# Attention and the sample's recurrent state, woven into fewer halves of the gate projections

## The chip, the cores and the metric

The kernel runs on one core of a Trainium2 chip. The metric is the time of one launch on the device in microseconds; for one core this is the core's own time. The time before is the median of three runs. The profile shows one further execution of the same program, with its own time.

## The reference: one decoder layer for a prompt and a sample

One layer is computed for a prompt of 512 tokens and for a sample of 8 sequences with 4 tokens each, both with the same weights, all in f32. Cut to its steps:

```python
z = x @ w_in + b_in                       # one projection, columns split among all mixers
qm, km, vm, og, ig, fg, qs, ks, vs, ga, gb = split(z)
h, C, n, m = mlstm_mix(...)               # recurrent matrix memory, 4 heads of 128 x 256
ya = head_norm(h) * sigmoid(og)
yb, k, v   = swa(...)                     # sliding window of 128, 16 query and 4 key heads of 64
mix = (sigmoid(ga) * (ya @ w_a) + sigmoid(gb) * (yb @ w_b)) @ w_out
x = LN1(alpha*x + mix)
x = LN2(alpha*x + moe(x))                 # 32 experts in 4 groups, two of them per token
x = LN3(alpha*x + sigmoid(x @ w_pg) * (p @ w_pp))
```

The prompt begins with an empty memory; the sample brings eight states C of 4 x 128 x 256 and windows of keys and values, and returns them updated. In local attention a query of the prompt sees its own block of 128 keys and the one before it (the first block sees itself alone), with a bias and a sink in the softmax.

## The kernel before

**Jobs.** A dense product with a weight matrix is cut into jobs of 256 columns. A job's weights come in one DMA of 1 MB (`fetch`, line 727) into `raw` and are split by ACT and DVE into a rounded part `wH` and a rest `wL` (lines 592 and 593, `split_from`). Three matmuls with f32r operands (`three`, lines 709 to 711) stand for one f32 product. In a "column" job each of two units holds 128 columns, and its product runs over the tokens in two halves, 0 to 255 and 256 to 543 (the second has the 32 sample tokens too), with 24 matmuls per half into a PSUM tile `pj`. After each half `done` moves the result out: for ga and gb DVE (line 881) takes the first half and ACT (line 879) the second, into `sigA` and `sigB`. The weights of a unit are split while the unit before it runs. ga and gb are four jobs each, so together 8 jobs, 16 units, 32 halves. Afterwards come the jobs of w_a, w_b and w_out.

**Weaving.** `stream` is a generator that yields after every half. `weave(upto, (generator, rate), ...)` advances it half by half; after each half every other generator gets its rate added to a counter and is resumed once for each whole number in it. So a rate of 2.6 writes 2.6 pieces of that work behind each half. When the jobs are done, what is left is written in turn.

**What is woven into ga and gb.** Two generators:

- `swa()`, the prompt's local attention: 16 units, for two pairs of key heads, four blocks of queries and two pairs of heads. For a unit, `stack` splits the queries (lines 1333, 1334), `scores` multiplies them with the keys into two PSUM tiles `tp` (lines 1350, 1352), DVE adds the bias and takes the maximum (line 1355), ACT takes the exponential (line 1367), and POOL divides by the sum (line 1373) in `lg`, which has two buffers. `values` turns the result on TensorE into a tile `nm` (line 1385), copies it to `pT` (lines 1388, 1390), multiplies it with the values into a tile `sp` (line 1397), and ACT copies the result over the queries (line 1399). The scores of a unit are written before the values of the one before it.
- `sample_mlstm()`, the sample's recurrence: a prelude, then for each of eight sequences b0 to b7 a load of its state `Cb` (512 KB, line 1419, on POOL's queue, two buffers), products with it into a tile `sp` (line 1490), four updates through tiles `tp` and `nm` (lines 1495 to 1498), and a store of the state (line 1501, POOL's queue). The ending turns the normaliser (line 1504), norms the result and multiplies it into the sample's columns of `ya` (lines 1512, 1514).

The PSUM tiles `tp`, `nm`, `sp` and `pj` have two buffers each, and are shared by all of these.

**What follows.** `early.close()` ends the pools of the projections' inputs, of the attention and of the sample's states. Then the sigmoids of `sigA` (line 1521) are written, then the split of `ya` into `yaH` and `yaL` (nine pieces on ACT and on DVE, lines 592 and 593 again), and then the jobs of w_a, which read them, with the sample's attention woven in.

**The order of the instructions.** The written order is not yet that of the engines. When the program is built, a planner plays it through with its own costs and deals the instructions out to the engines: an engine that is free takes, of those that are ready, the one written first. On the chip each engine keeps that order. Buffers of a pool with the same name are handed out in the written order.

Of the kernel before, what the change touches and what calls it, by code (L numbers as in the profile page):

```python
# [544 lines left out]
def tile_decoder_step(ctx: ExitStack, tc: tile.TileContext, *aps):  # L545
# [4 lines left out]
    def pool(name, bufs=1, side="left", space=None, stack=ctx):  # L550
        if space is None:
            return stack.enter_context(tc.tile_pool(name=name, bufs=bufs, side=side, reuse_waits="tile"))
        return stack.enter_context(tc.tile_pool(name=name, bufs=bufs, space=space))
# [260 lines left out]
    def weave(upto, *others):  # L814

        nonlocal flow
        others = [[g, rate, 0.0, True] for g, rate in others]
        while state["done"] < upto:
            next(flow)
            for o in others:  # L820
                o[2] += o[1]
                while o[3] and o[2] >= 1.0:
                    o[2] -= 1.0
                    o[3] = next(o[0], "end") != "end"
        if state["pending"]:
            state["pending"]()
            state["pending"] = None
        live = [o for o in others if o[3]]
        while live:
            live = [o for o in live if next(o[0], "end") != "end"]  # L830
# [134 lines left out]
    N_GA, N_GB, N_WA, N_WB, N_WO = 22, 26, 30, 34, 38  # L965
# [344 lines left out]
    sws = early.enter_context(ExitStack())  # L1310
# [202 lines left out]
        gated = ya[:, :, SEQ:].rearrange("p (h e) s -> p e h s", e=2)  # L1513
        dve.tensor_tensor(out=gated, in0=pt[:].rearrange("p e (h s) -> p e h s", h=MH), in1=gated, op=ALU.mult)

    weave(N_GB, (swa(), 2.6), (sample_mlstm(pool("smp", stack=sws)), 1.1))
    early.close()

    def sigmoids(g):
# [947 lines left out]
```

## Time and profile before

| | |
|---|---|
| median of three runs | 1100.4 us (1099.33 to 1101.43) |
| the profiled execution's own time | 1102.54 us |
| its span, first to last instruction | 1100.6 us |
| TensorE busy, matmuls | 1003.2 us, 91% |
| VectorE (DVE) / ScalarE (ACT) / GpSimd (POOL) busy | 512.0 / 369.0 / 255.7 us |
| granted TensorE clock, mean | 0.966 |
| DMA | 256.45 MB, mean 233 GB/s |

The span is cut into stages by what the jobs do. The projections of q, k, v and so on end at about 280 us; ga and gb run from there to about 430 us; w_a begins at 443.0 us; the experts' weights are streamed from about 558 us on, at some 426 GB/s in the middle of the experts' phase. The profile's lines have an engine, the line of the kernel, the operation, the tile written and the tiles read. TensorE's weight loads (PEld) overlap its matmuls. Behind an instruction stands how long its engine was idle before it and what it was waiting for.

### The profile page before, as it was taken

To read this page: it belongs to the slowest core of one execution; us is meant where nothing else is said; L and a number is where in the kernel's file an instruction comes from. 1 tells how busy PE (TensorE), PEld (TensorE's weight loads), DVE (VectorE), ACT (ScalarE), POOL (GpSimd) and SP (SyncE) were. 2 spreads that over 40 slices of the span, in tenths; PEclk is the share of its full clock that TensorE was granted. 3 is DMA by queue.
4 is the path that set the end of the run, shared out by engine and by line. 5 is a ranking of instruction groups with operands and counts; after the bars stand their busy time and mean duration, and the time that the engine had idled before them with its cause. 6 is when DMAs were issued, how large, how long until landed. Compare 5 with 4: busy or idle time off the path is not lost.

```text
span 1100.6 us, 26984 instructions
## 1 busy us (share of the span) xinstructions
PE 1003.2 (91%) x10269; PEld 823.1 (75%) x10270; DVE 512.0 (47%) x1308; ACT 369.0 (34%) x751; POOL 255.7 (23%) x385
## 2 busy tenths in 40 slices
PE   9999999999999998999999976875988888986987
PEld 8988999999988886899989634553556565654775
DVE  5555533645767765565566731111122222222696
ACT  5311224533677776523321311110111111223531
POOL 6000000501355555312410211111222222221011
PEclk9999999999999998999999988999899999999699
DMA  8321322222515423534379889999999999979701
GB/s 257 78 78 54 101 77 77 67 68 85 159 46 184 156 97 122 183 93 137 109 278 407 339 307 393 426 427 426 426 427 426 427 426 427 426 319 400 291 34 63
DMA packets 90892, 256.45 MB, mean 233 GB/s; under 512 B 11115, under 2 KB 58433, under 8 KB 70820
## 3 DMA queue, kind: packets, MB, share of 16 engines
q1 hardware_dynamic: 76036, 224.61, 52.9%
q0 software_dynamic: 10272, 27.21, 7.0%
q10 hardware_dynamic: 4512, 3.64, 1.1%
q8 instruction: 49, 0.80, 0.3%
q14 instruction: 23, 0.19, 0.1%
HBM read 241.89 MB, written 19.61 MB: 238 GB/s over the span
## 4 chain that ended last, share of the span: by engine, by line
PE 77%; DMA 7%; issue 6%; SPq 4%; DVE 4%; ACT 1%; POOL 1%; DVEq 0%; ACTq 0%; POOLq 0%
PE pj L709 14%; PE pj L710 14%; PE pj L711 13%; PE psG L306 13%; PE kept L318 6%; SPq L137 3%; DMA gu3b<-in_w_eu_dram 2%; DMA w<-in_w_pg_dram 2%; SPq L143 1%; PE sp L1397 1%; PE psX L298 1%; PE nm L1385 1%; PE sp L767 1%; DMA wg_in<-in_w_in_dram 1%; PE pp L2267 1%
## 5 line engine op out<-in xcount | busy, mean ns | idle before, releaser
L709 PE MATMUL pj<-xH,wH 128*128 128x256 f32 (+1 forms) x672 | 197.4, 294 | 0.0
L710 PE MATMUL pj<-xL,wH 128*128 128x256 f32 (+1 forms) x672 | 196.1, 292 | 0.0
L711 PE MATMUL pj<-xH,wL 128*128 128x256 f32 (+1 forms) x672 | 194.7, 290 | 0.0
L592 ACT CAST wH<-raw 128x1024 fp32r<-128x1024 f32 x76 | 79.6, 1048 | 200.5 <-PE pj L710 127.1
L709 PEld LDWEIGHTS pj<-xH,wH 128*128 128x128 f32 x672 | 126.5, 188 | 4.6 <-issue 3.7
L710 PEld LDWEIGHTS pj<-xL,wH 128*128 128x128 f32 x672 | 126.4, 188 | 2.2 <-issue 1.6
L711 PEld LDWEIGHTS pj<-xH,wL 128*128 128x128 f32 x672 | 126.2, 188 | 2.1 <-issue 1.9
L593 DVE TENSOR_TENSOR wL<-raw,wH 128x1024 fp32r<-128x1024 f32 x76 | 95.4, 1256 | 64.7 <-ACT wH L592 64.5
L474 DVE COPY xT<-xg 128x256 f32 x48 | 14.4, 299 | 224.6 <-PE psG L306 224.6
L306 PE MATMUL psG<-w,xT 128*32 128x256 f32 x1408 | 87.0, 401 | 28.6 <-issue 23.2
L306 PEld LDWEIGHTS psG<-w,xT 128*32 128x32 f32 x1408 | 53.6, 115 | 60.0 <-issue 39.0
L440 ACT ACTIVATE both<-psG 128x128 f32<-128x128 f32 x49 | 13.6, 278 | 242.9 <-PE psG L306 242.9
L1373 POOL TENSOR_SCALAR lg<-lg,sm 128x256 f32<-128x256 f32 (+1 forms) x64 | 59.0, 934 | 44.9 <-DVE sm L1370 34.7
L265 POOL DMA_INDIRECT ybuf<-ysb,idy x48 | 47.6, 991 | 43.6 <-POOL idy L262 39.6
L426 ACT ACTIVATE xg<-psX,gcol 128x128 f32 (+1 forms) x100 | 36.3, 467 | 51.4 <-PE psX L298 51.4
L709 PE MATMUL pj<-wH,xH 128*128 128x256 f32 x160 | 46.8, 292 | 1.0 <-DVE vs L923 1.0
L318 PE MATMUL kept<-w,hT 128*32 128x256 f32 x704 | 44.2, 390 | 2.5 <-DVE hT L479 2.5
L710 PE MATMUL pj<-wL,xH 128*128 128x256 f32 x160 | 44.4, 277 | 0.0
L711 PE MATMUL pj<-wH,xL 128*128 128x256 f32 x160 | 44.3, 277 | 0.0
L306 PE MATMUL psG<-gu3a,xT 128*32 128x256 f32 x480 | 30.7, 398 | 14.7 <-issue 6.7
L479 DVE STREAM_TRANSPOSE hT<-both 128x128 f32<-128x128 f32 x49 | 20.1, 409 | 45.4 <-PE kept L318 45.0
L306 PE MATMUL psG<-w2a,xT 128*32 128x256 f32 x384 | 26.6, 423 | 15.9 <-issue 12.8
(655 smaller groups left out, 2281.4 us busy)
## 6 DMA issues: line engine op xcount, KB each, us to landing
w<-in_w_eg_dram SPq DMA_DIRECT2D x24, 1024.0 KB, 24.9
w<-in_w_eu_dram SPq DMA_DIRECT2D x24, 1024.0 KB, 27.2
w<-in_w_ed_dram SPq DMA_DIRECT2D x24, 1024.0 KB, 27.4
raw<-in_w_in_dram SPq DMA_DIRECT2D x22, 1024.0 KB
r_p<-in_w_ed_dram SPq DMA_DIRECT2D x14, 1024.0 KB, 24.5
w2a<-in_w_eg_dram SPq DMA_DIRECT2D x7, 1024.0 KB, 20.0
w2a<-in_w_eu_dram SPq DMA_DIRECT2D x7, 1024.0 KB, 22.4
w2b<-in_w_eg_dram SPq DMA_DIRECT2D x7, 1024.0 KB, 23.6
```

The costliest lines, as they stand in the source:

```text
L137: return [eng.dma_start(out=W[s][half][:, i], in_=w[i][bass.ds(e, 1)].rearrange("a (p k) f -> (a p) k f", p=P)[:, ks]) for i in range(2)]
L265: gp.indirect_dma_start(out=ybuf.rearrange("t (q d) -> (t q) d", q=4), out_offset=bass.IndirectOffsetOnAxis(ap=idy[:, r:r + 1], axis=0), i ...
L306: m = pe.matmul(psG[32 * q:32 * q + 32], xT[:, k], W[s][half][:, :, kh, P * q:P * q + P], start=k == 0, stop=k == KD - 1)
L318: m = pe.matmul(out[32 * q:32 * q + 32], hT[:, 32 * k:32 * k + 32], W[s][2][k // 2][:, k % 2, 256 * q:256 * q + 256], start=k == 0, stop=k ...
L426: m = act.activation(out=out, in_=psX[:, k], func=AF.Identity, bias=gcol[:, 1, k:k + 1], scale=gcol[:, 0, k:k + 1])
L479: dve.transpose(out=hT[:].rearrange("p (r t) -> p r t", r=4), in_=h[:].rearrange("p (f r) -> p r f", r=4)).then_inc(S["ch"], 1)
L592: act.copy(out=H, in_=src)
L593: return eng.tensor_tensor(out=L, in0=src, in1=H.bitcast(F32), op=ALU.subtract)
L709: pe.matmul(out, lh(k), rh(k), start=start and i == 0, stop=False)
L710: pe.matmul(out, lh(k), rl(k), start=False, stop=False)
L711: pe.matmul(out, ll(k), rh(k), start=False, stop=stop and i == len(ks) - 1)
L1373: gp.tensor_scalar(out=lg[:, par, j, 0:nk], in0=lg[:, par, j, 0:nk], scalar1=sm[:, 2, par, j:j + 1], scalar2=None, op0=ALU.mult)
```

## The change

Only the two rates of one call are changed.

```diff
-    weave(N_GB, (swa(), 2.6), (sample_mlstm(pool("smp", stack=sws)), 1.1))
+    weave(N_GB, (swa(), 3.2), (sample_mlstm(pool("smp", stack=sws)), 1.2))
```

`swa()` yields 60 times and `sample_mlstm()` 21 times, so it takes 22 resumptions to run the sample to its end. Counted so, the last piece of attention was written behind half 24 and is now behind half 19 of 32, and the last of the sample was behind half 20 and is now behind half 19. (The change's own summary counts 23 and 22, and 19 and 20.) As the two rates grow by different shares, the order of the pieces among each other changes too. What is computed, the instructions, the buffers and the transfers stay as they were.

## The prediction

> **What bounds the kernel now.** I read the views in this order: the page for the shares, the busy time by stretch around the place of the change, TensorE's timeline where that stage ends, and the timelines of ACT and DVE at the same place. First the page.
>
> ```profile
> span 1100.6 us, 26984 instructions
> PE 1003.2 (91%) x10269; PEld 823.1 (75%) x10270; DVE 512.0 (47%) x1308; ACT 369.0 (34%) x751; POOL 255.7 (23%) x385
> ```
>
> TensorE is busy nearly throughout, so what counts is where it is not. By stretches (span, then busy time of each engine, the granted clock, DMA):
>
> ```profile
> 282.00:430.00 148.00, 148.00 (x1171) 129.86 (x1170) 98.35 (x336) 107.91 (x268) 76.52 (x100) 1.00 0.37 119
> 430.00:437.00 7.00, 2.60 (x20) 1.65 (x20) 3.27 (x11) 6.37 (x14) 4.03 (x5) 0.83 0.45 152
> 437.00:443.00 6.00, 4.44 (x20) 2.45 (x20) 0.82 (x2) 1.90 (x5) 6.00 (x12) 0.63 0.72 227
> 443.00:449.00 6.00, 5.63 (x30) 5.25 (x31) 6.00 (x11) 6.00 (x13) 3.22 (x6) 0.72 0.18 49
> ```
>
> From 282 to 430 us the gate projections ga and gb run with attention and states woven in, and TensorE never stands still. Then come 19 us in which it idles, and in which the clock falls to 0.63 and 0.72. TensorE's timeline says why (start, length, line, operation, idle time before):
>
> ```profile
> 430.20 0.29 PE L711 MATMUL pj<-xH,wL 128*128 128x288 f32 x1
> ...
> 433.36 0.65 PE L1397 MATMUL sp<-pT,vs 128*64 128x256 f32 x4 [1.33 <-DVE pT L1390]
> ...
> 440.44 1.57 PE L1397 MATMUL sp<-pT,vs 128*64 128x256 f32 x8 [0.57 <-DVE pT L1390]
> 443.02 0.38 PE L709 MATMUL pj<-yaH,wH 128*128 128x256 f32 x1 [1.01 <-ACT yaH L592]
> ...
> 449.38 0.30 PE L710 MATMUL pj<-yaL,wH 128*128 128x288 f32 x1
> ...
> 453.33 0.39 PE L709 MATMUL pj<-yaH,wH 128*128 128x256 f32 x1
> ...
> 456.29 0.29 PE L709 MATMUL pj<-yaH,wH 128*128 128x288 f32 x1
> ```
>
> The last gb matmul starts at 430.20. The last two attention units still have their transposes (L1385) and value products (L1397) to do, each behind another engine, until 440.44 + 1.57 = 442.0. Only then does w_a begin, at 443.02; its first half lasts until 449.38, 6.4 us, where a later half takes 456.29 - 453.33 = 3.0 us. What lies between is the split of ya:
>
> ```profile
> 442.06 0.37 ACT L1399 COPY qsT<-sp 128x256 f32<-128x256 f32 x1 [1.51 <-PE sp L1397]
> 442.35 4.57 ACT L592 CAST yaH<-ya 128x512 fp32r<-128x512 f32 x9
> 443.00 5.24 DVE L593 TENSOR_TENSOR yaL<-ya,yaH 128x512 fp32r<-128x512 f32 x9 [2.49 <-ACT yaH L592]
> ```
>
> Its casts follow on ACT right behind the attention's last copy: the tiles are opened after the attention's pools are closed. So the stage ends with a bare chain, and every microsecond by which attention (and the states, for yaL) end earlier is worth up to one, until gb itself is the end.
>
> **The change, part by part.** It adds no instruction, DMA or wait and removes none; two rates change what is written beside what. Counted from the generators' yields, attention has 60 pieces and the sample 22 resumptions. At 2.6 and 1.1 per half the last of them lie in halves 24 and 20 of 32; at 3.2 and 1.2 both lie in half 19.
>
> *Does the written place set the time?* Mostly not. One half takes 148.0 / 32 = 4.6 us. The scores of the last unit (call the units S0 to S15) are written in half 21, some 50 us before the end, but run in the last one. These are the first score matmuls of S4, S6, S9, S10, S11, S12, S14 and S15:
>
> ```profile
> 309.37 0.28 PE L1350 MATMUL tp<-kd,q 128*128 128x256 f32 x1
> 332.07 0.28 PE L1350 MATMUL tp<-kd,q 128*128 128x256 f32 x1
> 363.58 0.22 PE L1350 MATMUL tp<-kd,q 128*128 128x128 f32 x1
> 377.29 0.28 PE L1350 MATMUL tp<-kd,q 128*128 128x256 f32 x1
> 381.05 0.28 PE L1350 MATMUL tp<-kd,q 128*128 128x256 f32 x1
> 389.96 0.28 PE L1350 MATMUL tp<-kd,q 128*128 128x256 f32 x1
> 418.85 0.28 PE L1350 MATMUL tp<-kd,q 128*128 128x256 f32 x1
> 427.27 0.28 PE L1350 MATMUL tp<-kd,q 128*128 128x256 f32 x1
> ```
>
> The attention is about 50 us behind its place, so in any contest with the projections it already comes first; writing it still earlier wins nothing directly. What the rates do change is the order between units and states. Both take PSUM tiles with the same names (tp, nm, sp, two buffers each), handed out in written order, so a state written ahead of a unit holds that unit up. Written before: S4 b0 S5 S6 b1 S7 b2 S8 b3 S9 b4 S10 S11 b5 S12 b6 S13 b7 S14, the sample's ending, S15. After: S4 S5 b0 S6 b1 S7 S8 b2 S9 S10 b3 S11 b4 S12 b5 S13 S14 b6 S15 b7, ending. So b7 and the sample's ending move from ahead of S15 to behind it.
>
> *The price of a state in that queue.* S4 to S6 is two units and one state in 22.7 us, S9 to S11 the same in 17.5, mean 20.1. S11 to S14 is three of each in 37.8, 12.6 per pair. So a unit costs 20.1 - 12.6 = 7.5 and a state 5.1. Test: eleven units and eight states would make 123 us, and S4 to S15 took 117.9. Bounds: S10 and S11, with no state between them, are 3.8 us apart; if every unit cost that, a state would cost (117.9 - 41.8) / 8 = 9.5; if states rode free, 0. I take 5.1, nearest to the rows that mix both. The sample's ending lies between S14 and S15, 8.4 us apart: 8.4 - 7.5 = 0.9. S15 thus moves from 427.3 to 427.3 - 6.0 = 421.3, bounds 417 and 426.
>
> *The tail.* From S15 to the last value product it took 442.0 - 427.3 = 14.7, and 1.0 more to w_a. That gives 421.3 + 15.7 = 437.0 in place of 443.0: 6.0 us.
>
> *What now lies behind S15.* b7 and the ending, whose C_s store must land before yaL may use that memory. The nearest pattern (a unit, then a state straight behind it) is S8 with b3, the widest S12 with b6; S8's first score, then DVE's last update of b3, of b6 and of b7, ya's sample columns, and POOL's store of b3:
>
> ```profile
> 355.47 0.22 PE L1350 MATMUL tp<-kd,q 128*128 128x128 f32 x1
> 363.01 0.47 DVE L1498 SCALAR_TENSOR_TENSOR Cb<-Cb,win,nm 128x257 f32<-128x257 f32 x1
> 406.81 0.48 DVE L1498 SCALAR_TENSOR_TENSOR Cb<-Cb,win,nm 128x257 f32<-128x257 f32 x1 [1.02 <-PE nm L1497]
> 418.12 0.48 DVE L1498 SCALAR_TENSOR_TENSOR Cb<-Cb,win,nm 128x257 f32<-128x257 f32 x1 [0.40 <-PE nm L1497]
> 425.80 0.41 DVE L1514 TENSOR_TENSOR ya<-tp,ya 128x256 f32<-128x256 f32 x1
> 364.69 0.80 POOL L1501 DMA_DIRECT2D out_dram<-Cb  x1
> out_dram<-Cb POOLq DMA_DIRECT2D x8, 512.0 KB, 3.4
> ```
>
> Near pattern: update at 363.0, 7.5 after S8, store issued at 364.7, landed 3.4 later, 12.6 after S8. Behind a S15 at 421.3 that is 433.9, before the attention's end (436.0). The sample's columns follow their last update by 7.7: 421.3 + 7.5 + 7.7 = 436.5, needed only by w_a's second half. So this lies beside the tail and costs nothing; if the cover goes it costs what the slower rival below says. Behind a waiting load of a state on POOL's queue stands the normalising of the next unit (L1373); fewer states between units makes that rarer, and I count 0 for it.
>
> *How far it can go.* What TensorE did after 430.4 has to be done anyway, only earlier: eight transposes and eight value products for each of two units, and two small transposes. The chain of waits has their price at full clock (start, length, what):
>
> ```profile
> 410.39 0.22 PE nm L1385 x2
> 424.46 0.58 PE sp L1397 x4
> ```
>
> 18 x 0.11 + 16 x 0.145 = 4.3 us. So w_a cannot begin before 434.7.
>
> *w_a's first half.* 6.4 us now. DVE's nine pieces in 5.24 us set 8 x 0.58 = 4.7 for a first half that waits for its split at full clock. Saved between 0 and 1.7; the gap before w_a would shrink from 12.6 to 6.6 us with 4.3 of work in it, so I take 1.0.
> The Trainium skill (TensorE: Matmul & The Clock Gate, Part 1: The HAM clock gate) has the array's clock halved after an idle window of about 3.4 us and restored after as long of steady work. The trace agrees: 0.63, and still 0.72 in six well-filled microseconds. By that rule a gap of 2.3 us need not halve the clock at all, and the sum would be 7.7 in place of 7.0.
>
> *Sum:* 6.0 + 1.0 = 7.0 us off the profiled execution's 1102.5 (its span 1100.6 and 1.9 around it). The median of the runs, 1100.4, stands 2.1 below that execution; I take the same 7.0 off it: **1093.4**. Does it reach the end? TensorE is full in the last stretch of the dense part, and the experts' weight loads are first issued from memory that the dense part frees:
>
> ```profile
> 560.00:580.00 20.00, 20.00 (x177) 16.50 (x178) 12.27 (x25) 3.04 (x3) 0.00 (x0) 1.00 1.03 410
> 557.92 0.37 SPq L1760 DMA_DIRECT2D w<-in_w_eg_dram  x1
> ```
>
> So the whole later part moves with it; I count all of it.
>
> **The rivals.** *Hidden whole:* a state costs near its upper bound, or the written place counts after all; S15 comes at 417 or before, the attention ends before gb, w_a starts at 434.7 with its split done. 443.0 - 434.7 = 8.3, and the first half falls from 6.4 to about 3.9 (3.0 and eight transposes of 0.11): 10.8 us, 1089.6. For it: the 3.8 us spacing. Against: the lag of 50 us under either rate.
>
> *No effect:* states ride free and S15 stays near 426; the new tail ends at 441 or 442. 1099 to 1101. For it: each unit's own chain over two buffers could be all that paces. Against: 17.5 and 22.7 us for two units with a state, beside 3.8 for one without.
>
> *Slower, the sample becomes the last:* S15 stays at 427.3 and b7 behind it takes the widest pattern, S12 to b6's update: 406.8 - 390.0 = 16.8. Store issued 1.7 and landed 3.4 later: 449.2, and the split of ya starts there instead of at 442.35, 6.9 us later: 1107.3. It decides from the point where the store lands after 442.35, which at this spacing is S15 later than 420.4, at the near spacing (12.6) later than 429.7. For it: the ending, which was hidden ahead of S15, is now the last in line. Against: it needs both the unmoved S15 and the wide spacing.
>
> **How the numbers follow.** Forecast 0.52, hidden whole 0.15, no effect 0.14, slower 0.19. The likeliest's own range is 1090 to 1098 (S15 from 418 to 425). The range to record reaches past hidden whole and half-way into the slower case: 1088.5 to 1103. A measurement of this kernel can tell about 0.2%, 2.2 us, from no change. Faster: 0.52 + 0.15 = 0.67; same 0.14; slower 0.19.
>
> **What would show it.** Right: the last unit's scores start near 421 with b7's products behind them; the last L1397 ends near 436; the stretch from gb's last matmul to w_a's first is a few us with less than 3 idle; gb's last matmul comes slightly later than 430.2. Wrong: S15 unmoved relative to gb's end; yaH or yaL waiting for the store of Cb; TensorE idle inside ga and gb, because casts of weights stand behind denser attention; or a later stage that takes the gain back.

## The result, and the profile after

The changed kernel takes 1091.35 us (median of 12 runs, 1088.87 to 1097.63) against 1100.54 (12 runs, 1098.63 to 1103.94): a ratio of 0.9916, with a 95% interval from 0.9900 to 0.9932. The forecast was 1093.4. The profiled execution took 1091.46 us, its span is 1089.6, 11.0 under the one before.

The page of the changed kernel (share of the span and instructions per engine):

```profile
span 1089.6 us, 26983 instructions
PE 995.5 (91%) x10269; PEld 818.1 (75%) x10270; DVE 510.3 (47%) x1308; ACT 367.0 (34%) x749; POOL 253.8 (23%) x385
```

The same stretches (span, then busy time of each engine, granted clock, DMA), now up to the end of gb, for the first half of w_a, and for w_a behind that:

```profile
282.00:433.00 151.00, 150.56 (x1205) 132.42 (x1205) 99.93 (x344) 110.46 (x281) 79.37 (x105) 1.00 0.37 117
433.00:439.00 6.00, 5.46 (x28) 3.59 (x28) 5.46 (x10) 6.00 (x12) 5.68 (x11) 1.00 0.68 223
438.90:494.10 55.20, 55.20 (x506) 52.06 (x506) 30.34 (x50) 16.88 (x23) 10.00 (x17) 1.00 0.55 170
```

The bare 13 us in which the clock had fallen are gone: gb runs to 433, three microseconds longer than before, since the attention's work now lies under it, and w_a follows at full clock. TensorE's timeline has the first scores of S4, S14 and S15, the last value products, the last matmul of gb, then w_a and its second half:

```profile
306.25 0.28 PE L1350 MATMUL tp<-kd,q 128*128 128x256 f32 x1
...
396.50 0.38 PE L1350 MATMUL tp<-kd,q 128*128 128x256 f32 x1
...
408.58 0.28 PE L1350 MATMUL tp<-kd,q 128*128 128x256 f32 x1
...
431.45 1.08 PE L1397 MATMUL sp<-pT,vs 128*64 128x256 f32 x8
...
432.96 0.29 PE L711 MATMUL pj<-xH,wL 128*128 128x288 f32 x1
...
433.56 0.38 PE L709 MATMUL pj<-yaH,wH 128*128 128x256 f32 x1 [0.20 <-ACT yaH L592]
...
438.86 0.40 PE L709 MATMUL pj<-yaH,wH 128*128 128x288 f32 x1
...
551.37 0.31 PE L1783 MATMUL sp<-wrb,onesf 128*128 128x36 f32 x2
```

S15's scores moved from 427.27 to 408.58, 18.7 us, three times the forecast. Its last value product ends at 432.5, 23.9 behind its scores instead of 14.7. w_a starts at 433.56 instead of 443.02: 9.5 us, which is all there was, as gb's own last matmul is at 432.96. Of the sample, b7's last update, the store, ya's sample columns, and then the split:

```profile
417.89 0.86 DVE L1498 SCALAR_TENSOR_TENSOR Cb<-Cb,win,tp 128x257 f32<-128x257 f32 x2
419.46 0.80 POOL L1501 DMA_DIRECT2D out_dram<-Cb  x1 [0.39 <-issue]
423.50 0.42 DVE L1514 TENSOR_TENSOR ya<-tp,ya 128x256 f32<-128x256 f32 x1 [1.26 <-PE tp L1512]
433.54 5.24 DVE L593 TENSOR_TENSOR yaL<-ya,yaH 128x512 fp32r<-128x512 f32 x9 [4.26 <-ACT yaH L592]
```

So b7, though now behind S15, is stored at the same time as before (419.33) and has ten microseconds to spare.

The later part. Of the kernel before, the stretch of w_a behind its first half, in which TensorE was as full; then, from its timeline, transposes of the sample's attention inside w_a's first half, and the start of the experts' part:

```profile
449.00:503.40 54.40, 54.40 (x517) 51.81 (x516) 31.12 (x52) 14.91 (x21) 8.50 (x15) 1.00 0.50 158
```

```profile
448.36 0.60 PE L1593 MATMUL tp<-keep,kb 128*128 128x128 f32 x4
...
559.68 0.31 PE L1783 MATMUL sp<-wrb,onesf 128*128 128x36 f32 x2
```

The distance between the two kernels is 9.5 us at w_a's start, 10.5 at its second half (449.38 and 438.86), 9.3 at the start of w_b (503.45 and 494.14), and 8.3 where the experts' part begins. Before, w_a's waits had been filled with the sample's attention (line 1593 ran there); after, there are fewer waits, and that work lies behind them. At the end of the span the distance is 11.0. The last 2.7 are not put down to the change: a second profile of the changed kernel (below) has the same 551.3 at this mark and a span of 1087.5, so that the experts' part alone differs by 2.0 us between two executions of one kernel.

### The profile page after: what moved, and what is told of

Read it like the earlier page. It is cut to its first block, busy times and chain, and to the rows that moved or that the text cites. A ratio compares the mean times of both kernels' runs of the same rounds, so it can differ in the third digit from the quotient of the medians.

```text
span 1089.6 us, 26983 instructions
## 1 busy us (share of the span) xinstructions
PE 995.5 (91%) x10269; PEld 818.1 (75%) x10270; DVE 510.3 (47%) x1308; ACT 367.0 (34%) x749; POOL 253.8 (23%) x385
## 4 chain that ended last, share of the span: by engine, by line
PE 49%; issue 6%; DMA 5%; SPq 4%; DVE 3%; ACT 1%; POOL 0%; DVEq 0%; ACTq 0%; POOLq 0%
PE psG L306 14%; PE pj L709 6%; PE kept L318 6%; PE pj L710 6%; PE pj L711 6%; SPq L137 3%; DMA gu3b<-in_w_eu_dram 2%; DMA w<-in_w_pg_dram 2%; PE psX L298 1%; SPq L143 1%; PE po L711 1%; PE sp L1397 1%; PE po L709 1%; PE po L710 1%; PE nm L1385 1%
## 5 line engine op out<-in xcount | busy, mean ns | idle before, releaser
L306 PE MATMUL psG<-w,xT 128*32 128x256 f32 x1408 | 89.9, 412 | 31.2 <-issue 30.3
L253 POOL COPY idx<-tok 128x1 int32 (+1 forms) x12 | 2.2, 185 | 159.4 <-PE psX L298 159.4
## 6 DMA issues: line engine op xcount, KB each, us to landing
r_p<-in_w_ed_dram SPq DMA_DIRECT2D x14, 1024.0 KB, 22.5
```

The costliest lines, as they stand in the source:

```text
L306: m = pe.matmul(psG[32 * q:32 * q + 32], xT[:, k], W[s][half][:, :, kh, P * q:P * q + P], start=k == 0, stop=k == KD - 1)
```

## The experiments

In the table, times are those of each kernel's profiled execution; the ratio is that of the runs to the kernel before. "Sample" is the start of line 1514, the last that the sample writes into `ya`; "attention" is the end of the last value product.

| kernel | S15 | attention | sample | gb's last | w_a | ratio (95%) |
|---|---|---|---|---|---|---|
| before | 427.3 | 442.0 | 425.8 | 430.2 | 443.0 | 1 |
| changed | 408.6 | 432.5 | 423.5 | 433.0 | 433.6 | 0.9916 (0.9900 to 0.9932) |
| late_after_order | 408.6 | 432.6 | 423.5 | 433.0 | 433.6 | 0.9936 (0.9912 to 0.9960) |
| before_load_behind | 427.9 | 443.0 | 426.4 | 430.8 | 444.0 | 1.0006 (0.9980 to 1.0033) |
| before_b7_behind | 416.9 | 439.2 | 439.9 | 429.3 | 441.0 | 0.9971 (0.9949 to 0.9993) |
| after_b7_ahead | 423.6 | 440.4 | 423.5 | 430.7 | 441.5 | 0.9968 (0.9938 to 0.9999) |
| attention_rate | 410.8 | 433.0 | 445.3 | 431.6 | 449.1 | 1.0049 (1.0025 to 1.0073) |
| sample_rate | 429 | 448.5 | 425.6 | 426.9 | 449.6 | 1.0049 (1.0020 to 1.0077) |
| states_last | 387.8 | 410.3 | 478.7 | 421.8 | 479.8 | one run, 1136.5 us |
| faster_again | 405.7 | 428.8 | 425.3 | 434.0 | 434.3 | 0.9867 (0.9841 to 0.9894) |

**Order or place: late_after_order.** The two generators are resumed in the changed kernel's order by a helper, which is itself woven at 3.5 pieces per half: the order of after at the place of before.

```diff
-    weave(N_GB, (swa(), 2.6), (sample_mlstm(pool("smp", stack=sws)), 1.1))
+    def woven(a, b, ra, rb):      # a and b in the order of weave at rates ra, rb; one resumption per yield
+        ...
+    weave(N_GB, (woven(swa(), sample_mlstm(pool("smp", stack=sws)), 3.2, 1.2), 3.5))
```

> Units and states are resumed in the changed kernel's order, but written at the old rate, so that they end in half 24 of 32 instead of half 19. Order theory (only the order between units and states counts, the written place does not): S15's first score matmul near 408.6, w_a from 433.6, 1091.4 us, as in the changed kernel. Place theory (writing it earlier beside the projections is what helps): close to the kernel before, S15 near 427, w_a from 443, 1100 us. In between, both count.

In its timeline the same two instructions as in the changed kernel:

```profile
408.61 0.28 PE L1350 MATMUL tp<-kd,q 128*128 128x256 f32 x1
...
433.60 0.38 PE L709 MATMUL pj<-yaH,wH 128*128 128x256 f32 x1 [0.20 <-ACT yaH L592]
```

Within 0.04 us of the changed kernel's, and its interval holds the changed kernel's ratio. The written place does nothing here that these runs can tell; the order between the two chains is the change. The change's own words, "fewer halves", do not name what acts.

**A state's wait on POOL: before_load_behind.** Only the written order of two POOL instructions of a state is turned.

```diff
-            if b + 1 < SB:
-                load_state(b + 1)
             Cb = states.pop(b)
             ...
             gp.tensor_tensor(out=qm, in0=qw, in1=qmask[:, b, None, :].to_broadcast([P, MH, NS]), op=ALU.mult)
+            if b + 1 < SB:
+                load_state(b + 1)
             yield
```

> The kernel before, with the load of the next state issued behind the query product of the present one on POOL instead of ahead of it; TensorE's, DVE's and ACT's lists of instructions are unchanged. Theory A (a state's price is POOL's wait for the store of an earlier state to land, 3.3 and 3.6 us each in the trace of before, with the present state's query product queued behind it): states get shorter, S15 comes 6 us or more earlier, 1092 to 1095 us. Theory B (TensorE's list of instructions has no hole in ga and gb, so S15 stands where its place in that list puts it, whatever POOL waits for): S15 at 427.3 within 1 us, 1100.5 us within 1.5.

POOL's timeline still has the wait for the store, and S15 stands where it stood:

```profile
381.48 0.76 POOL L1419 DMA_DIRECT2D Cb<-in_state_mlstm_C_dram  x1 [3.27 <-DMA out_dram<-Cb]
...
427.87 0.28 PE L1350 MATMUL tp<-kd,q 128*128 128x256 f32 x1
```

The edit changed nothing on the chip: POOL runs the same order as before, the waits are as before (3.27 and 3.57 us), and the query products had been running ahead of them already (b6's at 374.8 here and at 374.4 in the kernel before, while the load of b6 itself waited until 381.5 and 380.9). So Theory A falls in the form in which it was put, for the query products did not wait for the load. That the wait costs something in another way is not excluded; a third buffer for the state, which would take it away, was not tried. Theory B's number came (427.9, 1.0006), but in a run that changed nothing it is no proof of it.

**The end of the order alone: before_b7_behind.** The order of before, except that the last state and the sample's ending are resumed behind S15's scores. The counts say how often attention and sample are resumed by turns; up to the "2, 1, 8" near the end (b7's load part, then eight pieces of attention with S14's and S15's scores) they are before's.

```diff
-    weave(N_GB, (swa(), 2.6), (sample_mlstm(pool("smp", stack=sws)), 1.1))
+    def in_turn(a, b, counts):    # resumes a and b by turns, so many times each
+        ...
+    turns = [2, 1, 3, 1, 2, 1, 3, 1, 3, 1, 2, 1, 3, 1, 2, 1, 3, 1, 3, 2, 2, 1,
+             3, 1, 2, 1, 3, 1, 3, 1, 2, 1, 3, 1, 2, 1, 8, 1, 3, 1, 3, 1, 1]
+    weave(N_GB, (in_turn(swa(), sample_mlstm(pool("smp", stack=sws)), turns), 3.5))
```

> The order of before, with one thing changed: the last state b7 and the sample's ending are resumed behind the last unit S15 (as in the changed kernel) instead of ahead of it. The prediction's step: b7 costs 5.1 and the ending 0.9, so S15 at 421.3, w_a from 437.0, 1094 us. Theory B: S15 stands at 28.5 halves of ga and gb in TensorE's list, against 30.3 before and 25.9 in the changed kernel, whose S15 ran at 427.3 and 408.6: so 4.25 us per half, S15 at 419.6, w_a from 435.3, 1093 us. Both hold if the sample is done in time: its ending stands behind the last projection here, and if it decides, the split of ya waits for the last store and the time is 1097 or more. The rest of what the change gained (to 1091.4) would then be the states spread among the earlier units.

Its timeline: the scores of S14 and of S15, the products of b7, the last value products, the sample's turn into `ya`, w_a:

```profile
410.54 0.28 PE L1350 MATMUL tp<-kd,q 128*128 128x256 f32 x1
...
416.88 0.28 PE L1350 MATMUL tp<-kd,q 128*128 128x256 f32 x1
...
427.50 0.64 PE L1490 MATMUL sp<-Cb,qm 128*32 128x257 f32 x8
...
437.27 1.97 PE L1397 MATMUL sp<-pT,vs 128*64 128x256 f32 x8 [0.57 <-DVE pT L1390]
439.18 0.69 PE L1512 MATMUL tp<-keep,v_s 128*128 128x128 f32 x2
...
441.03 0.58 PE L709 MATMUL pj<-yaH,wH 128*128 128x256 f32 x1 [0.74 <-ACT yaH L592]
```

POOL's timeline there, at b7's copy, and ACT's at the split of ya; then w_a's first 6 us as a stretch:

```profile
430.31 0.19 POOL L1500 COPY nT<-Cb 128x4 f32<-128x4 f32 x1 [5.47 <-DVE Cb L1498]
...
440.36 2.18 ACT L592 CAST yaH<-ya 128x512 fp32r<-128x512 f32 x4 [0.70 <-DVE ya L1514]
```

```profile
441.00:447.00 6.00, 5.73 (x32) 5.23 (x32) 5.99 (x10) 6.00 (x13) 3.75 (x8) 0.70 0.28 77
```

S14 moved from 418.85 to 410.54 and S15 from 427.27 to 416.88. So b7 in its old place held up S14 by 8.3 us and the ending held up S15 by another 2.1, together 10.4 where the prediction had 6.0. But the tail grew by 7.7, from 14.7 to 22.4. In part this is what had stood ahead of S15 and now stands between its scores and its values: S15's exponentials were done at 428.1, but POOL divided by their sum only from 431.5 on, behind b7's last update on DVE and its copy and store on POOL. That is not the whole, as states_last (below) has a tail of 22.5 without any state in it. And b7's own products moved from 414.77 to 427.50, so that now the sample is the last: ACT's split waits for it (0.70 behind DVE's `ya`). w_a comes 2.0 us earlier, not 6.0. Of two chains that share their tiles, one had been advanced at the cost of the other. And the clock in w_a's first 6 us is as low as before (0.70, and 0.72 before). Of the 2.0 us, 0.6 are left at the start of w_b (502.84 against 503.45).

**The rest alone: after_b7_ahead.** The changed kernel's order, with b7 and the ending put back ahead of S15.

```diff
-    weave(N_GB, (swa(), 2.6), (sample_mlstm(pool("smp", stack=sws)), 1.1))
+    turns = [3, 1, 3, 1, 3, 1, 3, 1, 4, 1, 3, 2, 3, 1, 3, 1, 3, 1,
+             4, 1, 3, 2, 3, 1, 3, 1, 3, 1, 4, 1, 3, 2, 2, 3, 8]
+    weave(N_GB, (in_turn(swa(), sample_mlstm(pool("smp", stack=sws)), turns), 4.4))
```

> The changed kernel's order, with b7 and the sample's ending put back ahead of the last unit S15. The prediction's prices: S15 6.0 later than 408.6, at 414.6, and with a tail of 15.7 to w_a still before the end of gb at 433: no change, 1091.4 us. Theory B: S15 stands at 29.2 halves in TensorE's list, so at 422.6; w_a from 438.3 instead of 433.6, 1096 us.

S14, b7's products, the sample's turn, S15, the last value product and w_a:

```profile
396.47 0.38 PE L1350 MATMUL tp<-kd,q 128*128 128x256 f32 x1
...
412.64 0.64 PE L1490 MATMUL sp<-Cb,qm 128*32 128x257 f32 x8
...
423.13 0.38 PE L1512 MATMUL tp<-keep,v_s 128*128 128x128 f32 x2
...
423.58 0.28 PE L1350 MATMUL tp<-kd,q 128*128 128x256 f32 x1
...
438.46 1.98 PE L1397 MATMUL sp<-pT,vs 128*64 128x256 f32 x8 [0.57 <-DVE pT L1390]
441.47 0.58 PE L709 MATMUL pj<-yaH,wH 128*128 128x256 f32 x1 [1.03 <-ACT yaH L592]
```

DVE's copy of the turned normaliser out of its tile `tp`:

```profile
420.49 0.28 DVE L1505 COPY n_in<-tp 32x128 f32<-32x128 f32 x1 [0.44 <-PE tp L1504]
```

Here the same two pieces hold up S15 by 15.0 us (423.58 against 408.58). In the changed kernel S15 had already run when b7 started, at 412.6; here b7 starts at the same 412.64, the ending's chain (turn, norm, turn back) lasts until 423.1, and S15 comes behind it. What S15 pays is not the sample's work but the time at which the sample's chain is done. How the two are tied was not taken apart. S15's first tile `tp` comes, in the written order, behind the turned normaliser's, and that was copied out by 420.8, 2.8 us before S15; so in the end S15's place in TensorE's list, which the planner gave it, held it, and not that tile. No run gave the two chains tiles of different names. The prediction's prices had said "no change" for this run; w_a came at 441.5. So each of the two parts of the change is worth little alone, 2.0 us of w_a's start for the swap at the end and 1.5 for the rest, and together 9.5.

**One rate at a time: attention_rate, sample_rate.**

```diff
-    weave(N_GB, (swa(), 2.6), (sample_mlstm(pool("smp", stack=sws)), 1.1))
+    weave(N_GB, (swa(), 3.2), (sample_mlstm(pool("smp", stack=sws)), 1.1))    # attention_rate
+    weave(N_GB, (swa(), 2.6), (sample_mlstm(pool("smp", stack=sws)), 1.2))    # sample_rate
```

> Only the attention's rate is changed, 2.6 to 3.2; the sample's stays at 1.1. The last unit S15 is then resumed ahead of b7 and the ending, as in the changed kernel, but the sample's states come later among the units. Theory C (both chains must be done by the end of gb; it is the later of the two that lies bare): S15 at 411 to 414, but the sample's ending behind the last projection and last of all, w_a from 438 to 442, 1096 to 1099 us. The prediction's prices (a state 5.1, a unit 7.5, the tail 14.7 behind S15, sample beside it): w_a at the end of gb, 433.6, 1091 us.

> Only the sample's rate is changed, 1.1 to 1.2; the attention's stays at 2.6. The states come earlier, all of them and the ending ahead of S14 or S15. Theory C: attention is the last, S15 at 428 to 431, w_a from 443 to 446, 1100 to 1103 us. The prediction's prices: the same states ahead of S15 as before, so S15 at 427.3 and 1100.5 us.

Each is slower than before, by 0.5%; both together are faster by 0.8%. With the attention's rate alone, attention is done at 433.0 as in the changed kernel, and then its timeline has (DVE's last update of b7, TensorE's wait for it, POOL's store, ACT's split, and w_a):

```profile
435.59 0.47 DVE L1498 SCALAR_TENSOR_TENSOR Cb<-Cb,win,nm 128x257 f32<-128x257 f32 x1
...
440.97 0.39 PE L1504 MATMUL tp<-keep,nT 128*32 128x128 f32 x1 [7.08 <-POOL nT L1500]
...
442.42 0.83 POOL L1501 DMA_DIRECT2D out_dram<-Cb  x1 [1.50 <-DMA bs<-relx]
...
448.45 1.66 ACT L592 CAST yaH<-ya 128x512 fp32r<-128x512 f32 x3 [9.46 <-DMA out_dram<-n_in]
...
449.12 0.58 PE L709 MATMUL pj<-yaH,wH 128*128 128x256 f32 x1 [2.23 <-ACT yaH L592]
```

This is the prediction's rival "the sample becomes the last", with a price that it had not seen: behind gb, POOL's queue already held the next section's transfers (lines 1566 to 1573), and the state's copy (line 1500, 440.71) and store stood behind them; the last update was done at 435.59 + 0.47 = 436.1, the store was issued at 442.4, and the split waited for the landing of the ending's n_s. With the sample's rate alone it is the attention that lies bare, its last product at 448.5. Theory C named the right chain as the last in both runs, but had w_a 3.6 to 11 us too early; for the attention's rate it had forecast a gain, and so the wrong sign, since it counted no such queue. The prediction's prices missed both.

**The units' own pace: states_last.**

```diff
-    weave(N_GB, (swa(), 2.6), (sample_mlstm(pool("smp", stack=sws)), 1.1))
+    weave(N_GB, (swa(), 3.2), (sample_mlstm(pool("smp", stack=sws)), 0.1))
```

> Attention at 3.2, the sample at 0.1, so that its states are written behind all units: no state stands between the units, and the states run one after another behind the last projection. A look at the pace of the units alone; the time itself must be long, since eight states lie bare. The prediction's unit of 7.5 us: S4 to S15 82.5 us, S15 near 389, all of attention done near 404. Theory C (a unit keeps its place among the projections at 22.7 halves of TensorE's list, against 25.9 in the changed kernel, and 3 to 4 us per half): S15 at 395 to 399, so 8 to 9 us per unit, and seven states between them then cost only 1 to 2 us each in the changed kernel. Time 1130 to 1200 us.

S4 and S15 in TensorE's timeline, and the stretch from the end of gb to w_a, in which the states run by themselves:

```profile
303.55 0.28 PE L1350 MATMUL tp<-kd,q 128*128 128x256 f32 x1
...
387.76 0.36 PE L1350 MATMUL tp<-kd,q 128*128 128x256 f32 x1
```

```profile
422.00:479.80 57.80, 20.47 (x102) 10.54 (x101) 23.48 (x60) 13.99 (x28) 24.35 (x49) 0.53 0.52 170
```

(387.76 - 303.55) / 11 = 7.66 us per unit: the prediction's 7.5 was right, Theory C's 8 to 9 was not. Between S4 and S15 the seven states of the changed kernel then cost (102.3 - 84.2) / 7 = 2.6 us each, and the eight with the ending of before (117.9 - 84.2) / 8 = 4.2; b7 alone in its old place cost 8.3. A state has no price of its own; it has one for each place. S15's 18.7 us can now be added up from three runs: 3.1 were won already at S4 (309.37 and 306.25; three pieces of the sample's prelude are written ahead of it instead of four), 10.2 between S4 and S15 by b7 and the ending (117.90 to 107.67 in before_b7_behind), and 5.3 there by the places of the seven other states (107.67 to 102.33). The tail, from S15 to the last value product, is 410.3 - 387.8 = 22.5 here, under gb and without a state in it.

The Trainium skill (TensorE: Matmul & The Clock Gate, Part 1: The HAM clock gate) says that the array's clock is halved when TensorE has been idle for a window, and is released by steady work. The runs agree: 0.53 in this stretch with 20.47 of 57.80 us busy, 0.70 behind the gaps of before_b7_behind, and 1.00 in the changed kernel, where 0.54 us of six are idle.

**A version that beats both: faster_still, split_by_columns, faster_and_split.** First the rates once more, then another order for the split of `ya`, then both.

```diff
-    weave(N_GB, (swa(), 3.2), (sample_mlstm(pool("smp", stack=sws)), 1.2))
+    weave(N_GB, (swa(), 4.0), (sample_mlstm(pool("smp", stack=sws)), 1.5))    # faster_still
```

```diff
-    for _ in split_tiles("ya", Z2, ya, "ya"):                                 # split_by_columns
-        pass
-    split_samples("ya", ya)
+    H, L = tiles["ya"] = tuple(Z2.tile([P, KD, NG], F32R, name="ya" + x, tag="split") for x in "HL")
+    for cols in (slice(0, 256), slice(256, NG)):
+        for k in range(0, KD, 2):
+            split_from(H[:, k:k + 2, cols], L[:, k:k + 2, cols], ya[:, k:k + 2, cols])
```

> Rates 4.0 and 1.5 in place of 3.2 and 1.2. Theory C: attention's last value product and the sample's ending both fall under gb with some 7 us to spare, so the split of ya (5.2 us on DVE) runs beside gb's last matmuls; w_a starts at the end of gb, 433 to 434, and its first half takes 3 to 3.5 us instead of the changed kernel's 5.3: 2 us under the changed kernel, 1089.3 against 1091.4 us. Rival: what the weave takes from the projections' casts and evictions leaves holes in TensorE inside gb, and nothing is won or 2 us are lost: 1091 to 1094.

> The changed kernel, with the split of ya made in another order: first the columns 0 to 255 of all eight row blocks, two blocks at a time, then the rest with the sample's columns. Theory: w_a's first half, which reads only columns 0 to 255, waits for DVE's pace over whole rows (8 pieces of 0.58 to 0.69 us); with four pieces of 0.69 it takes 3.7 instead of 5.3 us, its second half then 3.2 instead of 3.0: 1.4 us less, 1090 against 1091.4 us. Rival: the second half waits for the late pieces, and nothing is won: 1091.4.

> Rates 4.0 and 1.5 and the split of ya by columns. If the split lies under gb already at these rates, the columns add nothing: the same as at these rates alone, 1089.3 us. If it doesn't, 1 to 1.5 us less than these rates alone.

faster_still: 1087.34 us, ratio 0.9882 (0.9855 to 0.9909). split_by_columns: 1089.83, 0.9905 (0.9878 to 0.9932), no difference from the changed kernel's 0.9916. faster_and_split: 1087.21, 0.9887 (0.9861 to 0.9913), the same as the rates alone. The columns' rival was right: in its timeline w_a's first half is through its 24 matmuls in 3.7 us, as expected, but then

```profile
437.90 0.28 PE L711 MATMUL pj<-yaH,wL 128*128 128x256 f32 x1
439.42 0.37 PE L709 MATMUL pj<-yaH,wH 128*128 128x288 f32 x1 [1.24 <-DVE sigA L970]
...
434.44 4.50 DVE L593 TENSOR_TENSOR yaL<-ya,yaH 128x512 fp32r<-128x512 f32 x7 [4.26 <-ACT yaH L592]
438.85 0.42 DVE L970 TENSOR_TENSOR sigA<-pj,sigA 128x256 f32<-128x256 f32 x1
```

the second half waits until DVE has got through seven pieces and the first half's result. DVE has the same 5.2 us of work, and who waits for it has only changed.

**Side by side: changed_again, faster_again.** The changed kernel and the rates 4.0 and 1.5 on one chip.

> The changed kernel itself, beside the rates 4.0 and 1.5 on one chip. w_a's second half from 438.9, 1091.4 us if this chip is like the first, else by its ratio of 0.992 to the kernel before.

> Rates 4.0 and 1.5 once more, beside the changed kernel on one chip. Stage theory: w_a's second half 437.6 against 438.9, so 1.3 us under the changed kernel. Rival: the 4.0 us between the two medians of different calls is real and lies in the later part.

1093.25 us (1089.27 to 1094.40, ratio 0.9915, 0.9891 to 0.9939) and 1087.94 us (1086.88 to 1089.08, ratio 0.9867, 0.9841 to 0.9894). In the timelines of the latter, the attention's last copy and the split on ACT, w_a's start and its second half, and the start of the experts' part:

```profile
428.87 0.38 ACT L1399 COPY qsT<-sp 128x256 f32<-128x256 f32 x1 [0.42 <-PE sp L1397]
429.18 4.57 ACT L592 CAST yaH<-ya 128x512 fp32r<-128x512 f32 x9
...
434.26 0.37 PE L709 MATMUL pj<-yaH,wH 128*128 128x256 f32 x1
...
437.20 0.29 PE L709 MATMUL pj<-yaH,wH 128*128 128x288 f32 x1
...
549.60 0.31 PE L1783 MATMUL sp<-wrb,onesf 128*128 128x36 f32 x2
```

The split now begins under gb, w_a's first half takes 2.9 us without a wait, and the second half starts at 437.2 against 438.8: the stage theory's 1.3 us, here 1.6, and still 1.7 at the experts' part (549.6 and 551.3). The rest of the 5.3 us between the two medians lies behind it and was not found; between the two profiled spans (1086.1 and 1087.5) there are only 1.4.

## Why the prediction was right, and where it was not

The time, 1091.35, lies 2 us under the forecast, and the direction and the place of the gain were right. The path to the number was right at its two ends, not in the middle.

- *The written place doesn't count, the order does.* Right, and fully so: late_after_order.
- *A unit costs 7.5.* Right, 7.66.
- *A state costs 5.1, the ending 0.9, and S15 moves by 6.0 with bounds of 417 and 426.* This step failed. It made a price per state out of mean spacings and let nothing but b7 and the ending act on S15. Swapped alone, these two moved S15 by 10.4; in the changed kernel's order they would move it by 15.0, as S15 then runs only behind the end of the sample's chain. And they are not all of the 18.7 us: the swap leaves 8.3 of them (416.9 to 408.6), of which 3.0 lie ahead of S4 and 5.3 in the places of the other seven states among the units. The prediction had the new order before it, put nothing down for what is written ahead of S4, and gave the other seven states the same price in every place.
- *The tail stays 14.7.* This step failed too, in the other direction: 22.4 in the swap, 23.9 in the changed kernel, and 22.5 in states_last, where no state stands in it. The 14.7 was measured mostly behind gb's end; S13 of the kernel before, under gb, had taken 20.5 from its scores (405.9) to its last value product (426.4). Two misses, 12.7 too little for S15 and 9.2 too little for the tail, left 3.5: w_a at 433.6 instead of 437.0 (the earliest it could be had been put at 434.7, 1.1 too late). That they cancelled so far was luck.
- *b7 behind S15 lies beside the tail.* Right in the changed kernel (its store was issued 13 us before the split began), wrong for the swap alone, which the prediction had taken for the whole change: there the sample was the last.
- *w_a's first half saves 1.0.* 6.4 became 5.3, but by the start of w_b that microsecond was given back (9.5 at w_a's start, 9.3 at w_b's), because the sample's attention no longer fills waits there.
- *All of it reaches the end.* 8.3 of 9.5 reached the experts' part.
- The rival *hidden whole* comes nearest to what happened: it had w_a at 434.7 and 1089.6, and its reason, that a state's price reaches its upper bound, holds for b7 (8.3, bound 9.5), but not for the seven states of the new order (2.6 on average). It too had S15 at 417. The rival *the sample becomes the last* did not happen here, but did in attention_rate, one rate away: 1105.8 us, where the rival had 1107.3.

Why TensorE cannot repair a bad order by itself: the Trainium skill (PSUM — Partial Sum Buffer, Engine vs sequencer instructions) says that matmuls start and complete in program order. The runs fit this: in after_b7_ahead S15 runs 0.4 us behind the sample's turn (423.13 and 423.58), though in the changed kernel it ran 15 us earlier. What stays open is why a state costs 2.6 us on average in one order and 8.3 in one place of another. For b7 before, TensorE's rows suggest a chain: a value product of an earlier unit, b7's products right behind it, and only then S14:

```profile
414.18 0.65 PE L1397 MATMUL sp<-pT,vs 128*64 128x256 f32 x4
414.77 0.64 PE L1490 MATMUL sp<-Cb,qm 128*32 128x257 f32 x8
...
417.69 0.39 PE L1497 MATMUL nm<-v,kwm 96*128 96x258 f32 x1
```

S14's scores, which need none of these results, follow at 418.85, and without b7 they came at 410.54. For the other seven places no run tells, nor whether tiles of different names would have freed the one chain from the other.

## What to carry to other kernels

Where two chains are woven together and take buffers of the same names, ask of each unit which piece of the other chain is written ahead of it and when that one will be done; a mean price per piece misses it, and a swap may only move the delay to the other chain. Look at the end of both chains against the end of what they are woven into: here one rate alone cost 0.5%, and both together gained 0.8%. When both are hidden, the next thing in the row (the split of `ya`) can be hidden too, and only then is the stage at its floor.

## What the runs showed that was not expected

The two rates' effects do not add: 1.0049 and 1.0049 for each alone, 0.9916 for both. And a late tail costs more than its length: in attention_rate the transfers that the next section had queued on POOL stood ahead of the last state's store, which was issued 6.4 us after its data was ready.
